# A hybrid attention and expert-retrieval layer: 44 scatters a head instead of 48, dealt evenly over the activation items

## The chip, the cores and the metric

The kernel runs on one core of one Trainium2 chip. The metric is the time of one execution on the device in microseconds (us), as the median of several runs; beside it stands one execution that the hardware profiler recorded, whose times are used below.

## The reference

One layer over 528 tokens (16 learned ones and 512 of the input) of width 2048, all in float32. First come two groups of attention heads; then the expert retrieval with which this text deals. Every token picks, in each of 8 heads, 16 of 16384 experts by two lists of 128 keys, and adds up what they give:

```python
top_s, top_i = lax.top_k(s, PEER_TOPK)
cand_i = (top_i[:, :, 0, :, None] * N_KEYS + top_i[:, :, 1, None, :]).reshape(...)
best_s, best_j = lax.top_k(cand_s, PEER_TOPK)
idx = jnp.take_along_axis(cand_i, best_j, axis=-1)
g = jax.nn.softmax(best_s, axis=-1)
u_sel = jnp.take(u, idx, axis=0)
a = jax.nn.gelu(jnp.einsum('thkd,td->thk', u_sel, hb), approximate=False)
v_sel = jnp.take(v, idx, axis=0)
return jnp.einsum('thk,thkd->td', (g * a).astype(hb.dtype), v_sel)
```

## The kernel before

The first 1300 us are projections, attention and the search for the experts. The rest, written in one loop over `items`, retrieves them in two ways.

The first 160 tokens fetch the rows of their experts. A gather (`ahead`, L844, an indirect DMA that POOL issues) brings one row of 4096 numbers (an expert's `u` and `v`) for each of 128 tokens into `grf`; DVE takes the dot product with the token (L858), ACT makes a coefficient of it (L876, L877), and DVE adds the weighted second half to `acc` (L864). There are 160 such steps, two pieces of work each, and two buffers: the gather of step k + 1 goes into the buffer that step k - 1 leaves when its addition is done. `due` deals the pieces over the items.

The other 352 tokens (`TD`) go through all 16384 experts. In an item of kind A, one of 128 slices of `u` (1 MB, two loads `wr_u` on SP's queue) is cut into a high and a low part, in four pieces: ACT makes `wh_A` (L190), DVE `wl_A` (L191). PE runs 48 matmuls on them (L1032), ACT takes the GELU (L903), and SP stores the result in `a_scr`. Four buffers of each part hold one item, so that DVE can be no more than an item ahead of PE. 102 items of kind A follow each other, then 16 of kind D, which are the same but are multiplied at once with the gates, and then items of kind V, which weight the rows of `v`.

The gates are a table `g_scr` of 16384 x 352 numbers, nearly all of them zero. To fill it, DVE sums for every slot the weight that its expert has so far (`total`, L951, into `tot`), and POOL scatters one column of 128 such sums into the table by the positions in `dst` (L963, an indirect DMA too). A column stands for slot i of head h in block b of the tokens: 3 blocks of 128 partitions, 16 slots, 8 heads, 384 scatters. The 352 tokens don't fill 3 x 128 partitions: the first 32 partitions of block 0 are not theirs, and an iota sends them to places behind the table. The scatters of one head are free of each other; the first of a head waits until those of the head before it have landed. The table is read from item 99 on.

The generator `scatter` yields after each slot, with the totals of head h and the scatter of head h - 1 in one step, and an item takes 4 or 5 steps by turns (`NSC`). The orders of PE, DVE, ACT and SP in this loop are those in which the program is written; POOL's is not among them:

```python
fixed = {mybir.EngineType.PE, mybir.EngineType.DVE, mybir.EngineType.Activation, mybir.EngineType.SP}
with tc.manual_schedule(engines=fixed):
```

POOL's queue, scatters and gathers in one line, is set when the program is built, by a scheduler that takes what it holds to be ready. It then stands fixed.

Of the kernel before, what the change touches and what calls it, by code (L numbers as in the profile page):

```python
# [20 lines left out]
P = 128  # L21
# [3 lines left out]
D = 2048  # L25
# [3 lines left out]
TOPK = 16  # L29
PH = 8  # L30
X = 32
TD0 = P + X
TD = T - TD0
NDB = NTB - 1
NG = P // X
# [6 lines left out]
GATES = 1  # L42
WA = 1.9
JC = 16
LEAD = JC // 2 + 1
NSC = (4, 5)
AHEAD = 3


# [46 lines left out]
def hymba_peer(ctx: ExitStack, tc: tile.TileContext, xT, w_in, w_fl, b_fg, g_mix, g_q, g_k, g_merge,  # L96
               w_out, g_ffn, w_q, keysT, uT, uv, out):
    nc = tc.nc

    def pool(name, bufs=1, **kw):  # L100
# [38 lines left out]
                            base=0, channel_multiplier=1)  # L139
# [4 lines left out]
                            base=-P, channel_multiplier=-1)  # L144
# [3 lines left out]
                            base=0, channel_multiplier=1)  # L148
# [4 lines left out]
                            base=0, channel_multiplier=1)  # L153
# [70 lines left out]
    with ExitStack() as fctx:  # L224
# [9 lines left out]
        with ExitStack() as actx:  # L234
# [16 lines left out]
            for k in range(KD):  # L251
# [26 lines left out]
                b = big.tile([P, S], F32R, name=f"hl{k}", tag="hl")  # L278
# [364 lines left out]
        with ExitStack() as mctx:  # L643
# [65 lines left out]
            first = [project(w_out[c], mh, ml, [(0, T)], f"wo{c}", hfs=(0,)) for c in range(3)]  # L709
# [178 lines left out]
    def due(n, hold=False):  # L888
        done[1] += n
        want = 0 if hold else min(nwork, int(nwork * done[1] / (0.975 * (WA * (P - NAP - GATES - 1) + 2 * P))))  # L890
        r = range(done[0], max(want, done[0]))
        done[0] = r.stop
        return [gens[i + 1] for i in r]
# [5 lines left out]
    dst = gp.tile([P, NDB, P], I32, name="dst")  # L899
    tot = gp.tile([P, NDB, P], F32, name="tot")  # L900
    def act_out(j, ps, keep=False):
# [3 lines left out]
            return g  # L905
        nc.sync.dma_start(a_scr[j], g)

    def gates():
        e = gp.tile([P, NTB, P], F32, name="e")
        es = gp.tile([P, 2, NTB * PH], F32, name="es")  # L910
        ev = e.rearrange("p b (h k) -> p (b h) k", k=TOPK)
        nc.scalar.activation(e, res[:, :, 2, :], AF.Exp)
        nc.vector.reduce_sum(es[:, 0], ev, axis=AX.X)
        nc.vector.reciprocal(es[:, 1], es[:, 0])
        nc.vector.tensor_tensor(ev, ev, es[:, 1].unsqueeze(2).to_broadcast([P, NTB * PH, TOPK]), op=OP.mult)
        nc.vector.tensor_copy(g0, e[:, 0, :])
        nc.vector.scalar_tensor_tensor(ef, res[:, :, 1, :], float(P), res[:, :, 0, :], op0=OP.mult, op1=OP.add)
        nc.vector.tensor_copy(idx0, ef[:, 0, :])
        idxt = gp.tile([X, P], I32, name="idxt")
        nc.vector.tensor_copy(idxt, ef[:X, 1, :])  # L920
        for i in range(NG):
            for t, src in ((idx1, idxt), (g1, e[:X, 1, :])):
                nc.sync.dma_start(t[i * X:i * X + X], src[:, i * SL:i * SL + SL])
            nc.sync.dma_start(rxx[i * X:i * X + X], rx)
        for b in range(NDB):
            nc.vector.tensor_scalar(dst[:, b, :], ef[:, b + 1, :], float(TD), tcol[:, b:b + 1], op0=OP.mult, op1=OP.add)
        nc.gpsimd.iota(dst[:X, 0, :], pattern=[[1, P]], base=P * P * TD, channel_multiplier=P)
        return e

    act_out(JC, pa[0])  # L930
# [16 lines left out]
    def scatter():  # L947
        def total(h, b, i):
            s, w = h * TOPK + i, (h + 1) * TOPK
            junk = gp.tile([P, P], F32, name=f"junk{h}{b}{i}", tag="junk")  # L950
            nc.vector.scalar_tensor_tensor(junk[:, :w], ef[:, b + 1, :w], ef[:, b + 1, s:s + 1],  # L951
                                           gts[:, b + 1, :w], op0=OP.is_equal, op1=OP.mult,
                                           accum_out=tot[:, b, s:s + 1])

        slots = [(b, i) for b in range(NDB) for i in range(TOPK)]
        for h in range(PH + 1):
            head = []
            for b, i in slots:
                if h < PH:
                    total(h, b, i)  # L960
                if h > 0:
                    s = (h - 1) * TOPK + i
                    w = nc.gpsimd.indirect_dma_start(  # L963
                        out=g_flat, out_offset=bass.IndirectOffsetOnAxis(ap=dst[:, b, s:s + 1], axis=0),
                        in_=tot[:, b, s:s + 1], in_offset=None)
                    for x in head:
                        tc.declare_no_dep(w.ins, x.ins, reason="the experts of one head differ")
                    head.append(w)
                yield
# [4 lines left out]
    items = [("A", j) for j in range(JC + NAP, P)] + [("D", j) for j in range(JC)]  # L974
# [9 lines left out]

    def kind(t):
        return items[t][0] if 0 <= t < len(items) else ""

    def load_gates(t):
        if kind(t) not in ("R", "D"):
            return  # L990
        j = items[t][1]
        if kind(t) == "R":
            ga[j] = dn.tile([P, TD], F32, name=f"gb{j}", tag="gb", bufs=3)
            nc.sync.dma_start(ga[j], a_scr[j])
        gg[j] = dn.tile([P, TD], F32, name=f"gg{j}", tag="gg", bufs=3)
        nc.sync.dma_start(gg[j], g_tab[j])
# [90 lines left out]
    with tc.manual_schedule(engines=fixed):  # L1087
        sc = scatter()
        loaded = 0
        held = ()  # L1090
        for t in range(len(items) + 1):
            load_gates(t + 3)
            while t < len(items) and loaded < len(todo) and loaded <= rank[t] + AHEAD:
                load(todo[loaded])
                loaded += 1
            prev = items[t - 1] if t else ("",)
            turn = prev[0] == "V" and prev[1] % JC == JC - 1
            if turn:
                add_up(prev)
            if prev[0] == "A":  # L1100
                act_out(prev[1], ga.pop(prev[1]))
            if prev[0] == "D":
                ga[prev[1]] = act_out(prev[1], ga.pop(prev[1]), True)
                g = gated(prev[1])
                low(prev[1], *high(prev[1], g))
            if t == 0:
                cut_up(items[0], nc.gpsimd)
            if t == GATES:
                gts = gates()
            work = []  # L1110
            if kind(t) in ("A", "D") and t > GATES:
                work = due(WA) + [sc] * NSC[t % 2]
            elif kind(t) == "V":
                work = due(1, hold=items[t][1] % JC == JC - 1 and t < len(items) - JC)
            if nxt.get(t) is not None:
                cut_up(items[nxt[t]], nc.gpsimd if turn or kind(nxt[t]) == "V" and items[nxt[t]][1] % 4 == 2 else None, work)
            if kind(t) == "V" and items[t][1:] == (0, 0):
                hbx.close()
                vp = ppool["vp"] = ctx.enter_context(pool("vp", 1, side="right"))
                hb1 = vp.tile([P, D], F32, name="hb1")  # L1120
                ac1 = vp.tile([P, D], F32, name="ac1")
                nc.gpsimd.memset(ac1, 0.0)
                nc.sync.dma_start(ac1[:X], h_scr[P:])
                for i in range(NG):
                    nc.sync.dma_start(hb1[i * X:i * X + X], hx_scr)
                sets["x"] = (hb1, ac1, g1, idx1, dots1, coef1)
            if kind(t) == "V" and items[t][1] < JC and items[t][1] % 4 == 0:
                for _ in range(2):
                    b = len(accd)
                    accd.append(vp.tile([P, TD], F32, name=f"accd{b}"))  # L1130
                    nc.sync.dma_start(accd[b], ht_scr[b])
            if kind(t) == "V" and prev[0] == "V" and held:
                held = held[:1] + high(*held) if len(held) == 2 else low(*held) or ()
            if prev[0] == "R":
                if held:
                    low(*(held if len(held) == 3 else held[:1] + high(*held)))
                held = (prev[1], gated(prev[1]))
            for x in work:
                next(x, None)
            if t < len(items):  # L1140
                if done[0] == nwork and loaded == len(todo):
                    done[0] += 1
                    nc.sync.dma_start(out[:P, :], acc)
                    for i in range(1, NG):
                        nc.sync.dma_start(hb1[:X], ac1[i * X:i * X + X])
                        nc.vector.tensor_tensor(ac1[:X], ac1[:X], hb1[:X], op=OP.add)
                    nc.sync.dma_start(out[P:TD0, :], ac1[:X])
            if kind(t) in ("A", "D"):
                mm_u(items[t])
            elif kind(t) == "V":  # L1150
                mm_v(items[t])
        for half in range(2):
            put_out(half)
# [45 lines left out]
```

## Time and profile before

| | us |
|---|---|
| median of 3 runs | 3365.06 |
| lowest, highest | 3356.91, 3369.4 |
| the profiled execution | 3352.32 |
| its span, first to last instruction | 3350.6 |
| first matmul of the items of kind A | 1303 |
| first matmul of the items of kind D | 2202 |

The span of the profiled execution is 1.7 us shorter than its time, and its time is 12.7 us under the median of the other runs. Within it, an engine's busy time is the sum of its instructions; idle time before an instruction is put down to what ended it.

### The profile page before, as it was taken

What the parts mean: (1) busy time and instruction counts of PE and PEld (TensorE: products, weight loads), DVE (VectorE), ACT (ScalarE), POOL (GpSimd) and SP (SyncE); (2) the same over time, 40 slices, a digit from 0 to 9 for tenths busy, and PEclk for the clock granted to TensorE, in tenths of its full rate; (3) what the DMA queues carried; (4) which work ended last, traced back from release to release, by engine and by line L of the source; (5) the groups of instructions that cost most, each with busy time, mean ns of one, the idle gap of its engine ahead of it and who ended that gap; (6) DMA issues with size and microseconds to landing.
All of it is one profiled execution on the core that took longest, in us unless ns stands there. A gap on an engine that the chain in (4) does not pass through costs nothing.

```text
span 3350.6 us, 52860 instructions
## 1 busy us (share of the span) xinstructions
PE 3240.2 (97%) x19406; PEld 3046.7 (91%) x19406; DVE 2476.6 (74%) x4526; ACT 1349.3 (40%) x2762; POOL 1408.3 (42%) x974
## 2 busy tenths in 40 slices
PE   8999999999999999998989899999999999999998
PEld 6888888897888889998989899999999999999998
DVE  7555565666645997776767777677898889888885
ACT  5445554453333333333333333344333334433332
POOL 2000000003125866887878788112434434334332
PEclk9999999999999999999999999999999999999999
DMA  3332223222443235887888777888999999999994
GB/s 122 123 108 88 103 104 104 104 105 83 139 136 117 95 113 190 315 300 271 297 301 294 280 283 280 348 336 321 400 373 357 371 368 358 369 372 352 364 369 161
DMA packets 210661, 810.83 MB, mean 242 GB/s; under 512 B 35520, under 2 KB 89920, under 8 KB 189376
## 3 DMA queue, kind: packets, MB, share of 16 engines
q1 hardware_dynamic: 169184, 448.60, 37.8%
q0 software_dynamic: 41216, 358.85, 27.4%
q8 instruction: 152, 2.49, 0.3%
q14 instruction: 109, 0.89, 0.1%
HBM read 754.41 MB, written 52.10 MB: 241 GB/s over the span
## 4 chain that ended last, share of the span: by engine, by line
PE 75%; DMA 11%; issue 5%; DVE 5%; POOL 3%; ACT 1%; SPq 0%; DVEq 0%; POOLq 0%; ACTq 0%
PE pv L1046 21%; PE pa L1032 17%; DMA grf<-in_uv_dram,idx 7%; PE pj_wo L219 5%; PE pj_wq L219 5%; PE pj_sv L219 3%; PE pj_fv L219 3%; PE pj_sk L219 3%; PE pj_fk L219 3%; PE pj_fq L219 3%; PE pj_fg L219 3%; DMA wr_v<-in_uv_dram 2%; PE pa L219 2%; PE pj_sq L219 2%; POOL wl_V L191 2%
## 5 line engine op out<-in xcount | busy, mean ns | idle before, releaser
L1046 PE MATMUL pv<-ph,wl_V 128*128 128x352 f32 x2048 | 663.2, 324 | 18.2 <-POOL wl_V L191 13.5
L1046 PE MATMUL pv<-ph,wh_V 128*128 128x352 f32 x2048 | 660.1, 322 | 0.0
L1046 PE MATMUL pv<-pl,wh_V 128*128 128x352 f32 x2048 | 659.9, 322 | 0.0
L1032 PE MATMUL pa<-dh,wl_A 128*128 128x352 f32 x1632 | 545.8, 334 | 69.2 <-DVE wl_A L191 63.7
L963 POOL DMA_INDIRECT g_scr<-tot,dst x384 | 538.7, 1403 | 149.2 <-issue 88.8
L1032 PE MATMUL pa<-dh,wh_A 128*128 128x352 f32 x1632 | 543.0, 333 | 0.0
L1032 PE MATMUL pa<-dl,wh_A 128*128 128x352 f32 x1632 | 536.5, 329 | 0.0
L190 ACT CAST wh_V<-wr_v 128x512 fp32r<-128x512 f32 x512 | 310.9, 620 | 507.9 <-PE pv L1046 345.5
L858 DVE SCALAR_TENSOR_TENSOR grf<-grf,hbn 128x2048 f32<-128x2048 f32 x128 | 304.4, 2378 | 151.7 <-DMA grf<-in_uv_dram,idx 106.6
L1046 PEld LDWEIGHTS pv<-ph,wl_V 128*128 128x128 f32 x2048 | 385.5, 188 | 26.6 <-POOL wl_V L191 20.6
L190 ACT CAST wh_A<-wr_u 128x512 fp32r<-128x512 f32 x408 | 249.8, 617 | 378.8 <-PE pa L1032 297.5
L191 POOL TENSOR_TENSOR wl_V<-wr_v,wh_V 128x512 fp32r<-128x512 f32 x130 | 265.7, 2054 | 313.9 <-ACT wh_V L190 285.7
L1046 PEld LDWEIGHTS pv<-pl,wh_V 128*128 128x128 f32 x2048 | 385.6, 188 | 0.0
L1046 PEld LDWEIGHTS pv<-ph,wh_V 128*128 128x128 f32 x2048 | 385.6, 188 | 0.0
L1032 PEld LDWEIGHTS pa<-dh,wl_A 128*128 128x128 f32 x1632 | 314.9, 193 | 76.0 <-DVE wl_A L191 70.2
L191 DVE TENSOR_TENSOR wl_V<-wr_v,wh_V 128x512 fp32r<-128x512 f32 x382 | 285.6, 779 | 104.8 <-ACT wh_V L190 93.9
L191 DVE TENSOR_TENSOR wl_A<-wr_u,wh_A 128x512 fp32r<-128x512 f32 x404 | 277.4, 690 | 107.9 <-ACT wh_A L190 78.6
L844 POOL DMA_INDIRECT grf<-in_uv_dram,idx x128 | 184.9, 1445 | 394.3 <-DVE acc L864 346.6
L864 DVE SCALAR_TENSOR_TENSOR acc<-grf,coef,acc 128x2048 f32<-128x2048 f32 x128 | 309.1, 2415 | 14.9 <-ACT coef L877 12.0
L1032 PEld LDWEIGHTS pa<-dh,wh_A 128*128 128x128 f32 x1632 | 316.7, 194 | 0.0
L1032 PEld LDWEIGHTS pa<-dl,wh_A 128*128 128x128 f32 x1632 | 315.8, 193 | 0.0
L355 POOL TENSOR_TENSOR osq<-o 128x512 f32<-128x512 f32 x14 | 14.5, 1036 | 527.1 <-ACT o L349 527.1
(405 smaller groups left out, 6677.1 us busy)
## 6 DMA issues: line engine op xcount, KB each, us to landing
wr_u<-in_uT_dram SPq DMA_DIRECT2D x256, 512.0 KB
wr_v<-in_uv_dram SPq DMA_DIRECT2D x256, 512.0 KB
g_scr<-zero POOLq DMA_DIRECT2D x16, 1408.0 KB
gg<-g_scr SPq DMA_DIRECT2D x128, 176.0 KB
a_scr<-ga SPq DMA_DIRECT2D x112, 176.0 KB
gb<-a_scr SPq DMA_DIRECT2D x112, 176.0 KB
wr_wo<-in_w_out_dram SPq DMA_DIRECT2D x32, 512.0 KB
wr_wq<-in_w_q_dram SPq DMA_DIRECT2D x32, 512.0 KB
```

The lines of the kernel that those rows point to most:

```text
L190: nc.scalar.copy(hi, src)
L191: (lo_eng or nc.vector).tensor_tensor(lo, src, hi.bitcast(F32), op=OP.subtract)
L219: nc.tensor.matmul(ps[i][:, :hi - lo], wt[:, kk, :], ht[k][:, lo:hi], start=(k == 0 and n == 0), stop=(k == KD - 1 and n == 2))
L355: nc.gpsimd.tensor_tensor(sq, r, r, op=OP.mult)
L844: nc.gpsimd.indirect_dma_start(out=r, out_offset=None, in_=uv, in_offset=bass.IndirectOffsetOnAxis(ap=sets[st][3][:, s:s + 1], axis=0))
L858: nc.vector.scalar_tensor_tensor(r[:, :D], r[:, :D], 1.0, hb, op0=OP.mult, op1=OP.mult, accum_out=dt[:, c])
L864: nc.vector.scalar_tensor_tensor(ac, r[:, D:], cf[:, c], ac, op0=OP.mult, op1=OP.add)
L963: w = nc.gpsimd.indirect_dma_start(out=g_flat, out_offset=bass.IndirectOffsetOnAxis(ap=dst[:, b, s:s + 1], axis=0), in_=tot[:, b, s:s + 1] ...
L1032: nc.tensor.matmul(ps[:, :TD], wt[:, k % 4, :], ht[k], start=(k == 0 and n == 0), stop=(k == KD - 1 and n == 2))
L1046: nc.tensor.matmul(po["now"][n][:, :TD], w_, a, start=(jj == 0 and pi == 0), stop=(jj == JC - 1 and pi == 2))
```

## The change

The 12 first slots of block 2 and all of block 1 are scattered as before. The last 4 slots of block 2 move: the values of its 128 partitions, in four groups of 32, are copied into the 32 idle partitions of block 0, one group for each four of the 16 slots (`borrowed`). So a scatter of block 0 now carries 96 sums of its own and 32 of block 2, and a head takes 44 scatters. The positions are copied once, in `gates`, in place of the iota; the sums of a head are copied by four DMAs of SP when the last of its 48 totals is written. The blocks are taken in the order 1, 2, 0. In head 0 two totals go into a step; elsewhere a step has a scatter, and the moved slots have no step. The steps are spread over the items by `nsc`, 3 or 4 to an item, up to item 98.

```diff
-NSC = (4, 5)
+MOVED = TOPK // NG
...
+    def borrowed(t, heads, q):
+        return t[:X, 0].rearrange("p (h q m) -> p h q m", q=NG, m=MOVED)[:, heads, q]
...
-        nc.gpsimd.iota(dst[:X, 0, :], pattern=[[1, P]], base=P * P * TD, channel_multiplier=P)
+        for q in range(NG):
+            nc.sync.dma_start(borrowed(dst, slice(0, PH), q),
+                              dst[q * X:q * X + X, NDB - 1].rearrange("p (h s) -> p h s", s=TOPK)[:, :, TOPK - MOVED:])
...
-        slots = [(b, i) for b in range(NDB) for i in range(TOPK)]
+        slots = [(b, i) for b in (*range(1, NDB), 0) for i in range(TOPK)]
...
-            for b, i in slots:
+            for n, (b, i) in enumerate(slots):
                 if h < PH:
                     total(h, b, i)
+                if h < PH and n == len(slots) - 1:
+                    for q in range(NG):
+                        nc.sync.dma_start(
+                            borrowed(tot, slice(h, h + 1), q),
+                            tot[q * X:q * X + X, NDB - 1, None, h * TOPK + TOPK - MOVED:h * TOPK + TOPK])
+                if b == NDB - 1 and i >= TOPK - MOVED or h == 0 and n % 2 == 0:
+                    continue
...
+    first = items.index(("D", 0)) - 4
+    nscat = PH * (NDB * TOPK - MOVED) + NDB * TOPK // 2 + 1
+
+    def nsc(t):
+        return -(-nscat * (min(t, first) - GATES) // (first - GATES))
...
-                work = due(WA) + [sc] * NSC[t % 2]
+                work = due(WA) + [sc] * (nsc(t) - nsc(t - 1))
```

On POOL, in the middle of the stage, from gather 19 to gather 25, before (a gather is a row with `grf`, numbered by its step; a row with `g_scr` is so many scatters as stand behind the x):

```order
L844 DMA grf_19_16405<-in_uv_dram,idx0_8879 128x4096
L963 DMA g_scr_69<-tot_13074,dst_13073 5771264x1 x9
L844 DMA grf_20_16495<-in_uv_dram,idx0_8879 128x4096
L963 DMA g_scr_69<-tot_13074,dst_13073 5771264x1 x4
L844 DMA grf_21_16672<-in_uv_dram,idx0_8879 128x4096
L963 DMA g_scr_69<-tot_13074,dst_13073 5771264x1 x10
L844 DMA grf_22_16765<-in_uv_dram,idx0_8879 128x4096
L963 DMA g_scr_69<-tot_13074,dst_13073 5771264x1 x3
L844 DMA grf_23_16942<-in_uv_dram,idx0_8879 128x4096
L963 DMA g_scr_69<-tot_13074,dst_13073 5771264x1 x10
L844 DMA grf_24_17032<-in_uv_dram,idx0_8879 128x4096
L963 DMA g_scr_69<-tot_13074,dst_13073 5771264x1 x4
```

And POOL at the same gathers in the changed program, from gather 20 on:

```order
L844 DMA grf_20_16553<-in_uv_dram,idx0_8879 128x4096
L977 DMA g_scr_69<-tot_13074,dst_13073 5771264x1 x3
L844 DMA grf_21_16727<-in_uv_dram,idx0_8879 128x4096
L977 DMA g_scr_69<-tot_13074,dst_13073 5771264x1 x18
L844 DMA grf_22_16817<-in_uv_dram,idx0_8879 128x4096
L977 DMA g_scr_69<-tot_13074,dst_13073 5771264x1 x3
L844 DMA grf_23_16991<-in_uv_dram,idx0_8879 128x4096
L977 DMA g_scr_69<-tot_13074,dst_13073 5771264x1 x17
L844 DMA grf_24_17081<-in_uv_dram,idx0_8879 128x4096
L977 DMA g_scr_69<-tot_13074,dst_13073 5771264x1
L844 DMA grf_25_17260<-in_uv_dram,idx0_8879 128x4096
L844 DMA grf_26_17350<-in_uv_dram,idx0_8879 128x4096
```

Before, 9 or 10 scatters and 3 or 4 stand between gathers by turns; now 18, 3 and 17, and then none.

On SP, where head 1 ends, in the changed program (`wr_u` are the two loads of an item's weights, `a_scr` an item's store, `tot` the copies into the idle partitions):

```order
L1030 DMA wr_u0_47_15386<-in_uT_dram 128x1024
L1030 DMA wr_u1_47_15388<-in_uT_dram 128x1024
L906 DMA a_scr_70<-ga43_15390 128x352
L970 DMA tot_13074<-tot_13074 32x4 x4
L1030 DMA wr_u0_48_15480<-in_uT_dram 128x1024
```

The four copies stand between the store of one item and the loads of the next; the other rows are the old ones.

## Rows read from the trace of the kernel before

**Rows 1.** The page: busy time, share of the span, instructions.

```profile
PE 3240.2 (97%) x19406; PEld 3046.7 (91%) x19406; DVE 2476.6 (74%) x4526; ACT 1349.3 (40%) x2762; POOL 1408.3 (42%) x974
```

**Rows 2.** Stretches: their length, busy time, granted clock (PEclk), DMA share, GB/s.

```profile
core 0: us, PE busy (x) PEld busy (x) DVE busy (x) ACT busy (x) POOL busy (x), PEclk, DMA share, GB/s
1303.00:2202.00 899.00, 829.75 (x4898) 823.03 (x4897) 640.96 (x1378) 313.50 (x643) 631.87 (x453) 0.96 0.81 295
2202.00:3330.00 1128.00, 1109.70 (x6892) 1100.35 (x6891) 963.55 (x1108) 447.62 (x909) 416.09 (x225) 1.00 0.92 352
...
2150.00:2200.00 50.00, 50.00 (x308) 49.94 (x307) 34.04 (x38) 19.28 (x40) 6.17 (x4) 1.00 0.88 336
```

**Rows 3.** PE by line: 1303 to 2202, then 1450 to 2050.

```profile
L1032 PE MATMUL pa<-dh,wl_A 128*128 128x352 f32 x1632 | 545.8, 334 | 69.2 <-DVE wl_A L191 63.7 <-DVE junk L951 5.3
...
L1032 PE MATMUL pa<-dh,wl_A 128*128 128x352 f32 x1057 | 356.3, 337 | 57.2 <-DVE wl_A L191 51.8 <-DVE junk L951 5.3
```

**Rows 4.** DVE's waits, 1303 to 2202: sum, times, longest.

```profile
DVE grf L858 <- DMA grf<-in_uv_dram,idx: 94.4, 18, 9.5
...
DVE grf L858 <- issue: 44.9, 11, 8.5
```

**Rows 5.** POOL by line, 1450 to 2050: busy, mean ns, idle before.

```profile
L963 POOL DMA_INDIRECT g_scr<-tot,dst x298 | 420.0, 1409 | 109.7 <-issue 59.9 <-DVE junk L951 28.3 <-DMA g_scr<-tot,dst 14.0
L844 POOL DMA_INDIRECT grf<-in_uv_dram,idx x43 | 57.5, 1338 | 13.1 <-issue 8.2 <-DVE junk L951 3.7 <-DVE wl_A L191 0.6
```

**Rows 6.** POOL in order of time: start, length, what, idle before.

```profile
1914.88 0.97 POOL L963 DMA_INDIRECT g_scr<-tot,dst  x1 [0.30 <-issue]
1916.16 0.97 POOL L963 DMA_INDIRECT g_scr<-tot,dst  x1 [0.30 <-issue]
1917.44 0.98 POOL L844 DMA_INDIRECT grf<-in_uv_dram,idx  x1 [0.30 <-issue]
1918.72 3.02 POOL L963 DMA_INDIRECT g_scr<-tot,dst  x1 [0.30 <-issue]
...
1936.54 1.43 POOL L844 DMA_INDIRECT grf<-in_uv_dram,idx  x1 [0.31 <-DVE junk L951]
...
1943.39 0.98 POOL L844 DMA_INDIRECT grf<-in_uv_dram,idx  x1 [0.30 <-issue]
```

**Rows 7.** DVE in order of time: dot products (L858) and additions (L864).

```profile
1918.60 2.29 DVE L858 SCALAR_TENSOR_TENSOR grf<-grf,hbn 128x2048 f32<-128x2048 f32 x1 [8.46 <-DMA grf<-in_uv_dram,idx]
...
1924.26 2.34 DVE L864 SCALAR_TENSOR_TENSOR acc<-grf,coef,acc 128x2048 f32<-128x2048 f32 x1
...
1933.04 2.35 DVE L864 SCALAR_TENSOR_TENSOR acc<-grf,coef,acc 128x2048 f32<-128x2048 f32 x1
...
1947.66 2.29 DVE L858 SCALAR_TENSOR_TENSOR grf<-grf,hbn 128x2048 f32<-128x2048 f32 x1 [6.70 <-issue]
...
1961.28 2.29 DVE L858 SCALAR_TENSOR_TENSOR grf<-grf,hbn 128x2048 f32<-128x2048 f32 x1
```

**Rows 8.** Stretches of 2 us around that wait, columns as in rows 2.

```profile
1946.00:1948.00 2.00, 1.91 (x12) 1.61 (x10) 0.34 (x1) 0.00 (x0) 0.92 (x1) 1.00 1.10 405
1948.00:1950.00 2.00, 0.00 (x0) 0.00 (x0) 2.00 (x3) 0.00 (x1) 1.62 (x1) 1.00 0.96 400
1950.00:1952.00 2.00, 1.12 (x4) 1.12 (x5) 1.97 (x9) 1.87 (x5) 1.70 (x2) 0.74 0.92 371
1952.00:1954.00 2.00, 2.00 (x9) 2.00 (x8) 2.00 (x8) 0.13 (x1) 1.45 (x2) 0.50 0.78 269
```

**Rows 9.** SP's issues in order of time, 1337 to 1340.

```profile
1337.07 0.59 SPq L923 DMA_DIRECT2D idx<-idxt  x1
1337.70 0.59 SPq L923 DMA_DIRECT2D g<-e  x1
1338.33 0.59 SPq L924 DMA_DIRECT2D rxx<-rx  x1
1339.02 0.99 SPq L1009 DMA_DIRECT2D wr_u<-in_uT_dram  x2
```

**Rows 10.** SP's waits, 1450 to 2050: sum, times, longest.

```profile
SPq L1009 <- DVE junk L951: 500.1, 117, 13.1
```

More of the change, by code (lines that the diff above doesn't have):

```diff
@@ L1091, in hymba_peer @@
         for t in range(len(items) + 1):
+            if t == first + 1:
+                assert next(sc, None) is None and sc.gi_frame is None
             load_gates(t + 3)
```

## Prediction

> **What bounds the kernel now.** I read the page first: PE is busy 97% of the span and POOL 42% [rows 1], so anything that the change does to POOL counts only where PE waits. The table by stretches shows where that is. From 2150 on, PE passes 308 matmuls in 50 us, 0.1623 us each, so an activation item of 48 matmuls takes 7.79 us. The 102 items of kind A from 1303 to 2202 took 899 us, not 102 x 7.79 = 795 us: 104 us are lost there, and only there, since after 2202 PE is busy 98% at full clock [rows 2]. Of the 104 us, 69 are PE standing idle, nearly all until a `wl_A` piece is there [rows 3]; the other 35 are matmuls at the lower of its two clock levels (a mean granted clock of 0.96, and 0.50 just after a standstill) [rows 2, 8].
>
> The pieces `wl_A` are made by DVE, whose order is written out by hand, and DVE stands in front of a dot product on a gathered row: 94.4 + 44.9 us, 29 times [rows 4]. The gather that it waits for was late because of what stands ahead of it on POOL. From 1450 to 2050 POOL carried 298 scatters and 43 gathers: 478 us of work, and 0.30 us before each of the 341 instructions, 580 of 600 us; 14.0 us more are waits for an earlier scatter to land [rows 5]. So POOL is full. Its prices are 1.409 + 0.30 = 1.71 us for a scatter and 1.338 + 0.30 = 1.64 us for a gather. In this stretch PE did 3 x 1057 matmuls, 66 items [rows 3], so a gather comes every 66 / 43 = 1.54 items, or 12.0 us at PE's full pace.
>
> **A sum to test on before.** POOL's queue order, fixed when the program is built, is 57 gathers with 384 scatters between them, most often 4 and 9 by turns. I go from gather to gather: lateness grows by n x 1.71 + 1.64 - 12.0 and never falls below zero, and what exceeds the slack is lost to PE. The slack has two parts. A gather may start when the row buffer two gathers back is free: the one at 1936.54 follows an end at 1926.60 and was wanted at 1940.96 (1947.66 less 6.70 of waiting); the one at 1943.39 had its buffer free at 1935.39 and was wanted at 1954.58 (1961.28, less the 6.70 by which DVE had been put back). From a free buffer to the want that is 14.4 and 19.2 us; the row needs 11.1 us from gather to dot (1936.54 to 1947.66), so the lead is 3.3 to 8.1, say 5.7 us [rows 6, 7]. Then PE has pieces in hand: it ran till about 1947.9, 7.0 us past the want, and began again at 1950.9, 3.2 us after the late dot, so DVE may be 3.8 us late unpunished [rows 7, 8]. The slack is about 9 us. Summed so, before loses 71 us (384 x 1.71 + 57 x 1.64 - 57 x 12.0 = 66, and a little more where short turns waste time), with the 14.0 of landing waits 85. The trace has 104: the sum is some 20 us short, but near enough to compare two orders with.
>
> **The change, part by part.** Removed: 32 scatters, 32 x 1.71 = 55 us of POOL, and an iota of 0.26 us. Spread evenly that would make 352 x 1.71 + 57 x 1.64 = 695 us against 57 x 12.0 = 684 of PE, so nearly all of before's loss would go.
>
> Moved: the place of scatters in POOL's queue. The 16 scatters of block 0 now need the borrowed values, which are copied only after the last of a head's 48 totals, and the totals of block 0 come last. So for the 4 + 16 totals without a scatter, some 4.7 items at 4.24 totals an item (377 steps over 97 items, 48 totals in 44 steps), POOL gets only gathers; then 16 scatters fall due at once, and the next head's on their heels. The queue shows it. The scatters ahead of the gathers from the third on are now 8 15 5 1 3 18 3 16 3 0 0, 13 8 11 4 8 0 0, 2 3 18 3 17 1 0 0, 16 9 9 3 7 0 0, 6 12 14 3 9 0 0 0, 17 4 14 4 5 0 0, 7 12 8 11 3 3 0 0, 16: 352 over the same 57 gathers. Behind 18 scatters a gather comes 18 x 1.71 + 1.64 = 32.4 us after the one ahead, where DVE wants one every 12.0; queued behind that dot on DVE are the next items' pieces, for which PE waits. What POOL leaves unused at the zeros can't be drawn forward, since the values aren't there yet.
>
> The same sum with slack 9 gives, group by group, 32.8 + 14.6 + 24.9 + 18.0 + 14.8 + 19.8 + 14.5 + 8.0 = 147 us. The waits for landing stay (one at each head's first scatter). So after loses 147 - 71 = 76 us more than before.
>
> The bounds. Slack 5 (half of each part) makes it 184 - 77 = +107 us. The price of a scatter is the other unknown: beside a dot on DVE one took 3.02 us, in a wait of DVE's 0.97 [rows 6, 7]. If the surplus belongs to DVE's two long operations for each gathered row and not to the scatter, then a gather cycle costs n x 1.27 + 1.27 and at most 3.4 us once (298 x 0.44 + 43 x 0.37 = 147 us over 43 gathers). Summed so: 97 - 65 = +32 us; with slack 14 as well, -7. I take 76: flat prices with the traced mean return before's loss best, and a lump puts PE at its lower clock, which this sum prices only through the mean.
>
> A rule bears on this. In the Trainium skill, SBUF — State Buffer, "SBUF: two separate sides", a DMA issued from GpSimd can't write its descriptors while VectorE holds the port pair they share, and goes on when that operation ends; alone it needs none of that time. The trace agrees as to who stretches whom. By that rule the scatters in a lump, which mostly stand in a wait of DVE's, would be the short ones, and the sum would be the +32 above instead of +76.
>
> Added, and costed at little: 4 copies of positions and 8 x 4 copies of values on SP. The nearest rows are `idx`, `g` and `rxx`, 0.5 to 0.6 us of SP each when they don't wait [rows 9], so 36 x 0.6 = 22 us; SP waits 500 of 600 us for a free weight buffer anyhow [rows 10]. The first four stand ahead of the weights of item 31, which go out at 1339.02 [rows 9] with little to spare: up to +2.4 us, left out. The 384 totals on DVE stay; head 0's come two to a step. Gathers follow items, so the V stage keeps its work. The last total falls in step 333 of 377, at item 87 or so, and the last 16 scatters soon after; the first read of the table stands at item 99.
>
> **Rivals.** (1) Short scatters in the lumps, stretched by DVE's work alone: 3365 + 32 = 3397 us. For it: the 0.97 us rows while DVE waits. Against: with it before's own loss comes out at 65, further from the trace.
> (2) Less slack: PE loses both ends of a lump, 3365 + 107 = 3472 us.
> (3) The other side, faster. If a late gather cost nothing until it is over 20 us late, the lumps (18 x 1.71 + 1.64 - 12.0 = 20.4 us) would be ridden out and only the mean count: 695 - 684 = 11 us of loss for 71, about 60 us gained, 3305 us. For it: POOL really has 55 us less to do, and POOL is what is full. Against: the gather at 1936.54, 9.9 us later than its buffer allowed, did stop PE [rows 6 to 8].
> (4) No change: slack 14 and short scatters, -7 us, 3358 us.
>
> **How the numbers follow.** The profiled execution took 3352.3 us, 13 under the median of the three runs, 3365; the difference is put on the median: 3365 + 76, about 3440 us, alone 3415 to 3465. Chances: this 0.44, short scatters 0.22, less slack 0.14, no change 0.08, faster 0.12. A difference under 0.5% (17 us) is about what can't be told from none here. Slower is 0.80, the same 0.08, faster 0.12. The range leaves out the faster case and the far end of the slowest: 3360 to 3485.
>
> **What would show it.** Right: POOL's rows in lumps of 16 to 18 scatters with stretches of gathers alone; DVE's waits for a gathered row fewer but longer, over 10 us each, in all well over the 139 us of before; the A stage at some 975 us and a mean clock under 0.96; after it, all as before. The step on price is wrong if scatters in the lumps average 1.3 us; the slack if DVE's waits are long and PE's are not. The whole is wrong if the A stage falls under 880 us, with POOL no longer full.

## The result and the profile after

The changed kernel took 3459.64 us (median of 4 runs, 3459.13 to 3463.1) against 3363.46 for the kernel before (now the median of 4 runs): a ratio of 1.0289, 95% interval 1.0268 to 1.0309. That is 96 us slower where 76 were forecast.

The page of the changed kernel, its first rows, and the stretch of its A items (columns as in [rows 2]):

```profile
span 3457.4 us, 52688 instructions
...
PE 3257.9 (94%) x19406; PEld 3061.1 (89%) x19406; DVE 2482.4 (72%) x4526; ACT 1352.8 (39%) x2762; POOL 1299.0 (38%) x941
...
1303.90:2305.50 1001.60, 844.81 (x4894) 835.46 (x4893) 644.43 (x1380) 314.44 (x643) 540.25 (x421) 0.92 0.74 265
```

The stage takes 1001.6 us instead of 899 [rows 2]. It has POOL 92 us less busy, and PE further from its 795 us: 207 us lost instead of 104. The granted clock, 0.92, is lower with it.

PE and POOL by line in that stage, the answers to [rows 3, 5], and DVE's waits, to [rows 4]:

```profile
L1053 PE MATMUL pa<-dh,wl_A 128*128 128x352 f32 x1631 | 551.9, 338 | 153.2 <-DVE wl_A L191 147.2 <-DVE junk L958 5.6 <-issue 0.4
```

```profile
L977 POOL DMA_INDIRECT g_scr<-tot,dst x352 | 448.1, 1273 | 202.7 <-issue 88.7 <-DMA tot<-tot 51.7 <-DVE junk L958 50.7
L844 POOL DMA_INDIRECT grf<-in_uv_dram,idx x67 | 90.8, 1355 | 257.7 <-DVE acc L864 162.7 <-DVE junk L958 73.5 <-DVE idx L923 12.0
```

```profile
DVE grf L858 <- DMA grf<-in_uv_dram,idx: 188.8, 22, 18.4
...
DVE grf L858 <- issue: 30.5, 3, 11.0
```

PE's idle time has gone from 69 to 153 us, all but 6 of it until a `wl_A` piece. DVE waits for gathered rows 219 us in 25 waits, where it was 139 in 29: fewer and longer, 12 of them over 10 us, where the longest before took 9.5 [rows 4]. POOL is no longer full: it waits for DVE before gathers, for totals, and, which is new, 51.7 us for `tot`, the copied sums.

One head's end shows all of it. POOL in order of time (start, length, what, idle before):

```profile
1717.80 1.35 POOL L844 DMA_INDIRECT grf<-in_uv_dram,idx  x1 [6.36 <-DVE junk L958]
1721.61 1.00 POOL L977 DMA_INDIRECT g_scr<-tot,dst  x1 [2.46 <-DVE junk L958]
1725.77 1.19 POOL L977 DMA_INDIRECT g_scr<-tot,dst  x1 [3.16 <-DVE junk L958]
1731.98 1.97 POOL L977 DMA_INDIRECT g_scr<-tot,dst  x1 [5.03 <-DMA tot<-tot]
...
1752.18 0.97 POOL L977 DMA_INDIRECT g_scr<-tot,dst  x1 [0.30 <-issue]
1753.45 0.97 POOL L977 DMA_INDIRECT g_scr<-tot,dst  x1 [0.30 <-issue]
1754.72 0.98 POOL L844 DMA_INDIRECT grf<-in_uv_dram,idx  x1 [0.30 <-issue]
```

DVE's next two dot products, and SP's issue of the copies:

```profile
1738.55 2.28 DVE L858 SCALAR_TENSOR_TENSOR grf<-grf,hbn 128x2048 f32<-128x2048 f32 x1
...
1762.77 2.29 DVE L858 SCALAR_TENSOR_TENSOR grf<-grf,hbn 128x2048 f32<-128x2048 f32 x1 [15.55 <-DMA grf<-in_uv_dram,idx]
```

```profile
1721.52 0.44 SPq L906 DMA_DIRECT2D a_scr<-ga  x1
1722.00 2.41 SPq L970 DMA_DIRECT2D tot<-tot  x4
1726.12 3.14 SPq L1030 DMA_DIRECT2D wr_u<-in_uT_dram  x2
```

And PE over DVE's wait (columns as in [rows 2]):

```profile
1752.00:1754.00 2.00, 1.30 (x9) 1.01 (x7) 0.00 (x0) 0.00 (x0) 1.52 (x2) 1.00 0.02 1
1754.00:1756.00 2.00, 0.00 (x0) 0.00 (x0) 0.00 (x0) 0.00 (x0) 1.40 (x2) 1.00 0.01 0
...
1764.00:1766.00 2.00, 0.05 (x1) 0.05 (x1) 2.00 (x6) 0.87 (x3) 1.90 (x1) 0.50 0.01 0
1766.00:1768.00 2.00, 2.00 (x7) 2.00 (x8) 2.00 (x9) 1.01 (x3) 1.49 (x2) 0.50 0.58 170
```

The copies are issued by 1724.41, but the scatter that needs them starts at 1731.98, and 13 more follow it before the gather of 1754.72. That gather is 36.9 us behind the one before it, DVE stands for 15.6 us, and PE from 1753.3 to 1766, after which it runs at half its clock. In the wait the scatters take 0.97 us each, with 0.30 us between them: POOL loses no more time there, and it is late all the same. At the lump's end the DMA engines are nearly idle (0.01 to 0.02 of the time from 1752 to 1756).

### The profile page after: what moved, and what is told of

The parts are those of the page before. It is cut to its first block, busy times and chain, and to the rows that moved or that the text cites. A ratio compares the mean times of both kernels' runs of the same rounds, so it can differ in the third digit from the quotient of the medians.

```text
span 3457.4 us, 52688 instructions
## 1 busy us (share of the span) xinstructions
PE 3257.9 (94%) x19406; PEld 3061.1 (89%) x19406; DVE 2482.4 (72%) x4526; ACT 1352.8 (39%) x2762; POOL 1299.0 (38%) x941
## 5 line engine op out<-in xcount | busy, mean ns | idle before, releaser
L977 POOL DMA_INDIRECT g_scr<-tot,dst x352 | 448.1, 1273 | 202.7 <-issue 88.7
L858 DVE SCALAR_TENSOR_TENSOR grf<-grf,hbn 128x2048 f32<-128x2048 f32 x128 | 303.9, 2374 | 235.1 <-DMA grf<-in_uv_dram,idx 204.6
L191 POOL TENSOR_TENSOR wl_V<-wr_v,wh_V 128x512 fp32r<-128x512 f32 x130 | 252.8, 1955 | 315.2 <-ACT wh_V L190 309.9
L864 DVE SCALAR_TENSOR_TENSOR acc<-grf,coef,acc 128x2048 f32<-128x2048 f32 x128 | 306.6, 2396 | 12.6 <-ACT coef L877 11.4
```

The costliest lines, as they stand in the source:

```text
L191: (lo_eng or nc.vector).tensor_tensor(lo, src, hi.bitcast(F32), op=OP.subtract)
L858: nc.vector.scalar_tensor_tensor(r[:, :D], r[:, :D], 1.0, hb, op0=OP.mult, op1=OP.mult, accum_out=dt[:, c])
L864: nc.vector.scalar_tensor_tensor(ac, r[:, D:], cf[:, c], ac, op0=OP.mult, op1=OP.add)
L977: w = nc.gpsimd.indirect_dma_start(out=g_flat, out_offset=bass.IndirectOffsetOnAxis(ap=dst[:, b, s:s + 1], axis=0), in_=tot[:, b, s:s + 1] ...
```

## The experiments

All times are medians, and each ratio is against the kernel before on the same chip: 3366.58 us (19 runs) beside the first four runs below, 3359.64 us (9 runs) beside the last three. A ratio is estimated from the single runs and can differ by up to 0.003 from the quotient of two medians, so differences between runs are given by both.

**Scatters bound to the program's order.** In the changed kernel, each scatter is queued behind the last gather that the program has issued (an order on POOL's queue, no wait):

```diff
-                    w = nc.gpsimd.indirect_dma_start(
+                    with tc.issue_after(gathered[0].ins):
+                        w = nc.gpsimd.indirect_dma_start(
```

> The changed kernel, with each scatter bound behind the gather that stands ahead of it in the program: the 44 scatters of a head then stand 4 and 7 or 8 between gathers by turns, one head later, so that the copied values have long landed. If the lumps in POOL's order are what costs (theory 1), the stage of the A items loses little: 352 x 1.71 + 57 x 1.64 = 695 us of POOL against 684 of PE, so a stage of 800 to 850 us instead of 1002, and 3270 to 3320 us. If it is the copies themselves, their 36 DMAs on SP and the waits for them (theory 2), they are all still here and the time stays over 3420 us.

Measured: 3328.37 us, ratio 0.9878 (0.9843 to 0.9913). All 352 scatters, all copies and the even dealing are there, and the kernel is 1.2% faster than before, not 2.9% slower. So the order decides. The time is 8 us above the range that was expected, and the stage, 871 us, 21 above its own. Its stage and POOL's scatters:

```profile
1303.70:2174.30 870.60, 823.31 (x4895) 816.74 (x4894) 644.95 (x1380) 314.97 (x643) 600.98 (x421) 0.97 0.85 305
```

```profile
L979 POOL DMA_INDIRECT g_scr<-tot,dst x352 | 495.1, 1406 | 129.2 <-issue 100.3 <-DMA g_scr<-tot,dst 23.5 <-DMA grf<-in_uv_dram,idx 4.2
```

There is no waiting for `tot` any more, so it isn't the 36 small DMAs as such; and with DVE at work a scatter is back at 1.406 us.

**The same binding in the kernel before.**

> The kernel before with the same binding and nothing else: 384 scatters, 4 or 5 and 9 between gathers, one head later. POOL has as much to do as in the kernel before and in nearly the same turns, so by theory 1 the time is that of before, 3345 to 3380 us. A time well under that would say that the delay by a head, and not the number or the lumps, is what helps.

Measured: 3378.63 us, ratio 1.0027 (1.0005 to 1.0049). No gain, and by the interval a small loss; the stage takes 924.7 us, 26 more than before. With 384 scatters the binding, which delays them by a head, gives nothing; what it gives the changed kernel comes from 32 scatters less and no lumps. Between the two bound kernels, both without lumps, lie 50 us, where the 32 scatters are 55 us of POOL's work.

**No copies of sums.** The changed kernel without these lines:

```diff
-                if h < PH and n == len(slots) - 1:
-                    for q in range(NG):
-                        nc.sync.dma_start(
-                            borrowed(tot, slice(h, h + 1), q),
-                            tot[q * X:q * X + X, NDB - 1, None, h * TOPK + TOPK - MOVED:h * TOPK + TOPK])
```

> The changed kernel without the 32 copies of sums into the idle partitions (left out: the sums of the last 4 slots of block 2 don't reach their experts; their positions get other values). Number, dealing and order of the totals are as in the changed kernel, but the scatters of block 0 wait for nothing copied, and POOL's order comes out smooth after head 0: 3 or 4 and 8 by turns. Theory 1: the lumps are gone but for the first five, so 3290 to 3340 us. If the later place of block 0's totals or the even dealing were what costs, it would stay over 3420 us.

Measured: 3330.32 us, ratio 0.9866 (0.983 to 0.9902). With nothing to wait for, the scheduler lays the same scatters out smoothly after the first groups (8 15 6 15 2 11, then 3 or 4 and 8 or 9 by turns), and the kernel gains 36 us by the times and 45 by the ratio, of the 55 us of POOL's work that 32 scatters are. The place of block 0's totals and the dealing do no harm. Its stage:

```profile
1303.50:2169.90 866.40, 815.17 (x4896) 808.98 (x4895) 639.12 (x1378) 313.65 (x643) 603.70 (x420) 0.97 0.84 306
```

**The even dealing alone,** in the kernel before (`NSC` replaced by `nsc` for 48 scatters a head, two totals to a step in head 0):

> The kernel before with the even dealing alone: 48 scatters a head, blocks in the order 0, 1, 2, nothing copied, two totals to a step in head 0. POOL's order is 9 14 4 17 2 16 at first, then 4 and 9 by turns. Theory 1: as before, a little more for the lumps of the first head: 3360 to 3395 us. If the dealing were a cause of the loss, over 3420 us.

Measured: 3364.38 us, ratio 0.9993 (0.997 to 1.0015). The dealing alone changes nothing that can be measured.

**Half the lumps, no copies.** The run without copies, with the scatters of block 0 queued behind the gather at which their head's totals end:

```diff
+                if n == len(slots) - 1:
+                    ends[h] = gathered[0]
...
+                    with tc.issue_after(ends[h - 1].ins) if b == 0 else ExitStack():
```

> The changed kernel without the 32 copies of sums (left out as in the run without value copies), and with the scatters of block 0 bound behind the gather at which their head ends: one lump of 13 to 18 scatters a head and one gap, without any wait for copied data. Theory 1 (lumps alone): between the run without value copies (3330) and the changed kernel (3460); my sum over the groups with a slack of 5 us gives 116 us where it gives 34 and 184 for those two, so about 3400 us, 3375 to 3425. Theory 2 (the wait for the copies is the loss): 3330 to 3345 us.

Measured: 3385.25 us, ratio 1.0072 (1.0057 to 1.0087). Lumps that wait for no data cost 55 us over the smooth order by the times, 69 by the ratios (0.0206 of 3363). Both the sum's place for it (3400, 3375 to 3425) and its direction hold.

**All the lumps, no copies.** The run without copies, with every scatter bound behind the gather that it follows in the changed kernel:

```diff
+    place = [g for g, n in enumerate([0, 8, 15, 5, 1, 3, 18, ...]) for _ in range(n)]
...
+                    with tc.issue_after(gathered[place.pop(0)].ins):
```

> The changed kernel without the 32 copies of sums (left out as above), but with POOL's order bound to be that of the changed kernel, lump for lump: 352 scatters, 18, 3, 17 and zeros where it has them, with nothing copied to wait for. Theory 1 (the order alone): 3440 to 3465 us, as the changed kernel. Theory 2 (the copies' landing, 51.7 us of POOL's waiting in the changed kernel's trace, is a part or all of the loss): 3460 less up to 52, or more, so 3330 to 3410 us.

Measured: 3424.81 us, ratio 1.0192 (1.0176 to 1.0207). Neither theory alone. In its trace the order is that of the changed kernel but for three scatters, which stand one gather later. Its stage, PE and POOL:

```profile
1304.20:2270.70 966.50, 842.16 (x4896) 832.69 (x4895) 644.18 (x1380) 314.84 (x643) 559.18 (x421) 0.93 0.76 274
```

```profile
L1051 PE MATMUL pa<-dh,wl_A 128*128 128x352 f32 x1631 | 550.2, 337 | 120.6 <-DVE wl_A L191 112.7 <-DVE junk L960 5.3 <-DVE grf L860 1.3
```

```profile
L975 POOL DMA_INDIRECT g_scr<-tot,dst x352 | 466.6, 1326 | 133.0 <-issue 90.6 <-DVE junk L960 22.2 <-DMA g_scr<-tot,dst 16.3
```

The lumped order, without the copies, costs 95 us more than the smooth one by the times and 110 by the ratios (0.0326 of 3363); the copies and the waits for them bring the other 0.0097, 33 us. The 51.7 us of POOL's waiting for `tot` are gone from its row, and so are 33 of the 153 us of PE's idle time. The head's end that was shown above, with 16 scatters between the same two gathers, looks so here:

```profile
1708.47 1.35 POOL L846 DMA_INDIRECT grf<-in_uv_dram,idx  x1 [6.24 <-DVE junk L960]
1710.12 1.00 POOL L975 DMA_INDIRECT g_scr<-tot,dst  x1 [0.30 <-issue]
...
1737.37 1.36 POOL L846 DMA_INDIRECT grf<-in_uv_dram,idx  x1 [0.30 <-DVE junk L960]
```

The second gather comes 28.9 us behind the first, where the changed kernel took 36.9.

**Spread from the start.** The changed kernel with the order written out: the n-th scatter stands in step n + 3, while the totals of head 0, two to a step, put all totals half a head ahead; each scatter is bound behind the last gather.

```diff
+        for k in range(len(order) + LAG):
+            for h, b, i in totals[k] if k < len(totals) else ():
+                total(h, b, i)
...
+            if k >= LAG:
+                h, b, i = order[k - LAG]
...
+                with tc.issue_after(gathered[0].ins):
```

> The changed kernel with the order of scatters written out: each scatter three steps behind the step in which its number stands, while the totals run half a head ahead, bound behind the gather before it. 352 scatters over nearly all the A items, 3.6 an item, none late for its copies. Theory 1: POOL needs 7 x 1.71 + 1.64 = 13.6 us and 4 x 1.71 + 1.64 = 8.5 us by turns, 22.1 where PE takes 24.0, so PE hardly ever waits for it: 5 to 25 us under the run with the scatters in the program's order, 3300 to 3325 us.

Measured: 3297.86 us (5 runs, 3281.89 to 3309.54), ratio 0.9804 (0.9784 to 0.9825): faster than both kernels, and a little under what was expected. The profiled execution is the slowest of the five (3309.54). Its stage, and PE by line:

```profile
1303.60:2148.80 845.20, 813.57 (x4894) 809.29 (x4894) 645.04 (x1380) 315.43 (x643) 605.25 (x421) 0.98 0.87 314
```

```profile
L1064 PE MATMUL pa<-dh,wl_A 128*128 128x352 f32 x1631 | 537.8, 330 | 27.3 <-DVE wl_A L192 25.7 <-DVE grf L860 1.4
```

The same 352 scatters and the same copies leave PE 27 us idle before the matmuls on `wl_A`, where the changed kernel has 153. Of the 50 us that the stage still loses, a part is the first scatter of a head, which waits for the landing of those before it, with gathers behind it:

```profile
1721.10 1.89 POOL L988 DMA_INDIRECT g_scr<-tot,dst  x1 [0.30 <-issue]
1729.30 2.46 POOL L988 DMA_INDIRECT g_scr<-tot,dst  x1 [6.31 <-DMA g_scr<-tot,dst]
1732.07 1.37 POOL L846 DMA_INDIRECT grf<-in_uv_dram,idx  x1 [0.30 <-DVE junk L960]
```

## Why the prediction was right

**The bound.** POOL's queue set the pace of the A stage before: with 32 scatters less and a smooth order the kernel gains 1.3% (no copies) or 1.2% (bound to the program's order), with the old number and the binding nothing.

**The step that decided,** that the scatters of block 0 fall due in a lump at a head's end and hold up the gathers behind them, held in sign and place, and was shown by itself: the same 352 scatters with nothing copied take 3330 us in a smooth order and 3425 us in the lumps. Rival 3, that a gather may be 20 us late unpunished, falls: the sum with 20 us of slack puts the half lumps 37 us under before (23 against 60), and they came 24 us over it. Rival 4 falls with the interval. Rival 2, PE losing both ends of a lump, has 107 us from the lumps; without the copies they cost 65.

**The size.** The forecast was 76 us; 96 came. Two terms were mis-sized, one each way, so the 20 us by which it was out are less than the 33 that it left out.

The wait for the copies was not in the sum. "Added, and costed at little" priced the copies by SP's time to issue them and left out what POOL waits for their landing: 51.7 us in six waits, the longest 11.7, of which 33 us reach the end (3460 against 3425). It is the waits and hardly the issuing: with all the copies and no wait for them the run in the program's order takes 3328 us, the one without copies 3330. The wait stands at the head of POOL's queue, with gathers behind it: exactly what makes a wait on this queue dear.

The lumps, on the other hand, were priced somewhat too high. Over before they cost 1.92%, 65 us, not 76. The price of a scatter is a part of that: in the groups of 13 or more between two gathers one took 1.35 us on average in the run with the lumps and no copies, and 1.31 in the changed kernel, not 1.409. The prediction's own sign for a wrong price was 1.3 us, so this step stands at its edge.

Rival 1 was right on who stretches whom: in that run 97 of the 352 scatters ran while DVE did nothing, 0.97 us each, and those beside one of DVE's two long operations took 1.79 us. The rule of the Trainium skill named with it (SBUF — State Buffer, "SBUF: two separate sides") agrees with that in direction. But the lumps don't stand mostly in a wait of DVE's: DVE was at work in 72% of their scatters' time in that run. The 16 scatters between 1708.47 and 1737.37 took 28.9 us with the gather, which is the flat price (16 x 1.71 + 1.64 = 29.0) and not rival 1's (16 x 1.27 + 1.27 + 3.4 = 25.0); and with the 9 us of slack its sum gave 32, half of the 65. With its price and a slack of 5 us, both ends that the prediction named, the sum comes to some 60 to 65. That is a fit made afterwards, and the slack was measured in no run by itself; so how much of the missing 11 us belongs to the price and how much to the slack stays open.

**What the sum is worth.** It put the orders that were run in their right places, smooth, half the lumps, all the lumps; the stage's own loss was 24 to 76 us above it (172 for 147 in the run with all the lumps and no copies, 104 for 71 before, 76 for nearly 0 in the changed kernel bound to the program's order). As a difference from before it held within 20 us for the lumps, the half lumps, the run without copies and the one spread from the start, and missed by 28 and 43 us in the two runs bound to the program's order; why is open. As a loss by itself it would not have held.

**The rest** came as forecast. Of the 106.8 us between the two profiled spans, 103 lie in the A stage: the stages after it carry next to nothing.

## What to carry to other kernels

Where one in-order queue carries both a bulk of small work and the few instructions that somebody waits for, count what stands between those few, not the total: 8% less bulk cost 1.9% in lumps, 2.9% with the wait for the copies at their head, and gained 2.0% spread out. A new data dependence on part of such a bulk moves all of it in a queue that a scheduler fills, so print the queue's order before and after; if it has lumped, bind the bulk to the places where it is wanted. And a copy put into a chain costs its landing at the head of whoever waits for it, however short its issue; where its reader stood well behind it, as in the two runs with the changed kernel's scatters bound to the gathers, no such wait showed.

## What the runs showed of the hardware

Four copies of half a KB each, issued within 2.41 us by 1724.41, let the scatter that needs them start only at 1731.98, and over the stage such waits came to 51.7 us. Two loads of weights and a store were issued just ahead of them, and two more loads behind; whether these hold them up was not tried.

While DVE stood in a wait, scatters went out every 1.27 us (0.97 and a gap of 0.30) one after another, and from 1752 to 1756 the DMA engines were used for 0.01 to 0.02 of their time: what limits a row of such scatters is POOL's issuing, not their transfer.
